# Attention output with features on partitions: values as loaded operand, two query tiles of scaled and turned weights as moving operand

## The chip, the core and the metric

The kernel runs on one core of one Trainium2 chip. The metric is the device time of a whole execution in microseconds. Before the change three runs took 3046.93, 3048.78 and 3053.7 us, median 3048.78.

The names of the engines in the profile are PE (TensorE: matrix products and transposes), PEld (its weight loads), ACT (ScalarE), DVE (VectorE), POOL (GpSimd) and SP (the engine that issues most transfers).

## The reference, cut to what matters

The program is a two-layer backbone over 512 tokens of width 1024 with a context of 256 tokens. Layer 0 mixes tokens by attention of 8 heads, layer 1 by pooling; each layer is followed by a product-key expert network, which takes most of the time. The change is in the attention alone:

```python
def one(qblk):                       # a block of 128 queries, all heads
    sc = einsum('bqhd,bkhd->bhqk', qblk, k) * scale      # 768 keys: 512 tokens + 256 of context
    p = softmax(sc, axis=-1)
    return einsum('bhqk,bkhd->bqhd', p, v)               # v: 128 features a head
y = concat_of_heads @ mla_w_o[j]     # (512 x 1024) @ (1024 x 1024)
x = layernorm(alpha * x + gate * y)
```

## The kernel before

**Stages.** `mla` (L212) first computes the latent projections, the rotary keys and the values `vt` (tokens on partitions, 6 chunks of 128 tokens, 1024 columns: 8 heads of 128 features). Then comes the attention loop, then the output projection with normalisation (`o_turn`, `y_tile`, `y_norm`), then the routing of the expert network.

**The attention loop** runs over 32 steps, head by head, four query tiles t of 128 queries to a head. The order of the work is the order of the code: each engine takes its instructions in the order in which they are issued here, and waits at an instruction whose operands are not there. For step i the code issues:

- `turn_p(i)`: six transposes of the unnormalised weights P (128 queries x 768 keys) into PSUM (`pt`), and one ScalarE copy to `PT` (keys on partitions);
- `scores(i+2)`: ten products into a PSUM tile `s` (two buffers), then on VectorE the row maximum into `mx` and its scaling;
- `projection(i)`: for query tiles 3, 0 and 1, a part of the next head's queries or keys (PSUM tile `qk`), split by ScalarE (high part) and VectorE (low part) into `qn` or `kn`; query tile 2 has none;
- `weigh(i)`: six f32 products PT x values into `po` (128 queries x 128 features), the reciprocal of the row sum, and a ScalarE copy to O with that factor;
- `soft(i+2)`: on ScalarE the exponential P of the scores, with the row sum in `mx`;
- for query tile 2 `head_split(h+2)`: the weights `hw` of the head after next are split, high part on ScalarE, low part on VectorE; the first product that needs them is that of query tile 3;
- `unit()`, mostly two to a step: a modulation dot of 128x1024 on VectorE (line L229, tile `wmod`), whose end lets SP fetch a later one.

**Behind the loop**, `o_turn(t)` transposes a query tile of O (queries on partitions) in eight products to features on partitions, and ScalarE and VectorE split it into the two halves OT. `row_form` makes a row `grow` of the gate. `y_tile` multiplies OT by the output weights `wo`, which are split on the way in the first tile. In the loop over t, `o_turn(t + 1)` stands ahead of `y_tile(t)`.

The functions that the change touches, with the lines of the profile:

Of the kernel before, what the change touches and what calls it, by code (L numbers as in the profile page):

```python
# [10 lines left out]
F32 = mybir.dt.float32  # L11
# [5 lines left out]
AF = mybir.ActivationFunctionType  # L17
# [4 lines left out]
D = 1024  # L22
S = 512
C = 256
L = S + C
NT = S // 128
H = 8
# [24 lines left out]
def body(ctx: ExitStack, tc, A):  # L52
    nc = tc.nc
# [6 lines left out]
    ident = const.tile([128, 128], F32, name="ident")  # L60
# [29 lines left out]
    def mm(out, lhsT, rhs, first, last):  # L90
        nc.tensor.matmul(out, lhsT, rhs, start=first, stop=last)  # L91
# [7 lines left out]
    def split(hi, lo, src):  # L99
        nc.scalar.copy(hi, src)  # L100
        nc.vector.tensor_tensor(lo, src, hi.bitcast(F32), op=OP.subtract)  # L101
# [110 lines left out]
    def mla():  # L212
        scale = DK ** -0.5
# [27 lines left out]
        vt = m2.tile([128, L // 128, D], F32, name="vt")  # L241
# [205 lines left out]
        for tiles in ((4, 5), (0, 1, 2, 3)):  # L447
            for t in tiles:
                if t < NT:
                    b = zB[t // 2][:, t % 2 * 256:t % 2 * 256 + 192]  # L450
# [105 lines left out]
                wo[h] = mO.tile([128, D], F32, name="wo", bufs=4)  # L556
                nc.sync.dma_start(wo[h], A["mla_w_o"][h * 128:(h + 1) * 128, :])

        O = mO.tile([128, NT, D], F32, name="O")
        at = Pool("att")  # L560
        pa = Pool("psT", space=PS)
        steps = [(h, t) for h in range(H) for t in range(NT)]
# [17 lines left out]
        def soft(i):  # L580
            p, mx = Sx.pop(i), sums[i]
            P = Px[i] = at.tile([128, L], F32, name="P", bufs=3)
            nc.scalar.activation(P, p[:, :L], AF.Exp, scale=scale, bias=mx[:, 1:2], accum_out=mx[:, 2:3])

        def turn_p(i):
            P = Px.pop(i)
            pt = pa.tile([128, 1024], F32, name="pt")
            for k in range(L // 128):
                nc.tensor.transpose(pt[:, k * 128:(k + 1) * 128], P[:, k * 128:(k + 1) * 128], ident)
            PT = PTx[i] = at.tile([128, L // 128, 128], F32, name="PT", bufs=2)  # L590
            nc.scalar.copy(PT.rearrange("p a b -> p (a b)"), pt[:, :L])

        def weigh(i):
            h, t = steps[i]
            PT, mx = PTx.pop(i), sums.pop(i)
            po = pa.tile([128, 512], F32, name="po")[:, :128]
            for k in range(L // 128):
                mm(po, PT[:, k, :], vt[:, k, h * 128:(h + 1) * 128], k == 0, k == L // 128 - 1)
            nc.vector.reciprocal(mx[:, 3:4], mx[:, 2:3])
            nc.scalar.activation(O[:, t, h * 128:(h + 1) * 128], po, AF.Copy, scale=mx[:, 3:4])  # L600

        def projection(j):

# [5 lines left out]
        for i in range(2):  # L609
            scores(i)  # L610
            soft(i)
        done = 6
        for i, (h, t) in enumerate(steps):
            turn_p(i)
            if i + 2 < len(steps):
                scores(i + 2)
            projection(i)
            weigh(i)
            if i + 2 < len(steps):
                soft(i + 2)  # L620
            if t == 2:
                head_split(h + 2)
            if 6 <= i < 10:
                wo_load(i - 6)
            want = 6 + min(74 - NL, (i + 1) * (74 - NL) // 32)
            while done < want:
                unit()
                done += 1
# [36 lines left out]
        def o_turn(t):  # L665
            OT[t] = [wk.tile([128, H, 128], R32, name=f"OT{k}", bufs=2) for k in range(2)]
            for half in range(2):
                p = tr.tile([128, 512], F32, name="tr")
                for k in range(4):
                    c = half * 4 + k  # L670
                    nc.tensor.transpose(p[:, k * 128:(k + 1) * 128], O[:, t, c * 128:(c + 1) * 128], ident)
                split(*[x[:, half * 4:half * 4 + 4, :].rearrange("p a b -> p (a b)") for x in OT[t]], p)

        xn = {}

# [902 lines left out]
```

## Time and profile before

| | us |
|---|---|
| median of three runs | 3048.78 |
| the profiled execution | 3045.26 |
| its span, first to last instruction | 3043.5 |
| TensorE busy | 2944.9 (97%) |
| VectorE busy | 2397.6 (79%) |
| ScalarE busy | 1216.7 (40%) |
| GpSimd busy | 960.9 (32%) |

All times within an execution are counted from the start of the span. A row of the timeline gives start, duration, engine, line, operation, output and inputs with shapes and count; in square brackets stands how long the engine had been idle before it, and what it waited for. A product of f32 operands is listed as two passes (the products of the split halves, type fp32r in the program, as one); durations of products overlap, so the distance of two starts tells what one costs. A small ScalarE row ACTIVATION_READ_ACCUMULATOR behind an exponential is the moment at which its row sum is stored. The granted clock is a share of full speed: 1.00 is the 2.4 GHz level, 0.50 the 1.2 GHz level.

### The profile page before, as it was taken

Reading aid. Unit: us, or ns where it says so; the run is one execution under the profiler, and the core shown is the slowest. Engines: PE = TensorE matmul, PEld = TensorE weight load, DVE = VectorE, ACT = ScalarE, POOL = GpSimd, SP = SyncE. Lnnn points to the kernel's source line nnn. Section 1 sums busy time; section 2 is a strip of 40 time slices with the busy share of each in tenths; the row PEclk is TensorE's granted clock in tenths of the full one; section 3 lists DMA queues with packets and bytes.
Section 4 is the critical chain, followed back from the end, with each engine's and each line's share of the span. In section 5 each row is a group of like instructions: output and inputs, shape, how many; then the busy total and the mean of one; then the engine's idle time right before and its main releaser. Section 6 shows DMA issues by size and latency. Waiting matters only on the chain.

```text
span 3043.5 us, 44992 instructions
## 1 busy us (share of the span) xinstructions
PE 2944.9 (97%) x15364; PEld 2509.6 (82%) x15364; DVE 2397.6 (79%) x4921; ACT 1216.7 (40%) x2267; POOL 960.9 (32%) x1047
## 2 busy tenths in 40 slices
PE   7999998999999999999998999899999999999997
PEld 4787757889999999999986755888999999999986
DVE  7667798977778888888876378896787888888886
ACT  3444234544433333333334333554433333333333
POOL 0000344004344444444412134102344444444430
PEclk9999999999999999999999999999999999999998
DMA  7366522675699999999982321577499999999993
GB/s 260 111 227 214 203 68 73 257 256 186 223 323 324 332 332 319 332 328 324 347 304 82 145 91 59 186 259 231 146 321 325 332 324 331 327 328 324 322 338 137
DMA packets 351479, 756.98 MB, mean 249 GB/s; under 512 B 30336, under 2 KB 121600, under 8 KB 347792
## 3 DMA queue, kind: packets, MB, share of 16 engines
q1 hardware_dynamic: 270768, 423.21, 41.4%
q0 software_dynamic: 77024, 280.56, 26.6%
q10 hardware_dynamic: 3456, 50.33, 4.3%
q8 instruction: 120, 1.97, 0.3%
q14 instruction: 111, 0.91, 0.1%
HBM read 695.26 MB, written 58.72 MB: 248 GB/s over the span
## 4 chain that ended last, share of the span: by engine, by line
PE 83%; DVE 9%; issue 3%; ACT 2%; DMA 2%; POOL 0%; SPq 0%; ACTq 0%; DVEq 0%; POOLq 0%
PE acc L96 12%; PE acc L97 11%; PE acc L95 11%; PE mm L91 7%; PE pA L95 5%; PE pA L97 5%; PE pA L96 5%; PE pG L97 5%; PE pG L95 5%; PE pG L96 5%; DVE eq L1198 2%; DVE oh L1193 1%; PE po L91 1%; DVE lo L101 1%; PE s L91 1%
## 5 line engine op out<-in xcount | busy, mean ns | idle before, releaser
L101 DVE TENSOR_TENSOR lo<-raw,hi 128x512 fp32r<-128x512 f32 x1024 | 669.1, 692 | 276.0 <-ACT hi L100 273.9
L95 PE MATMUL acc<-hi,WH 128*128 128x512 f32 x1536 | 598.1, 389 | 5.4 <-ACT WH L1152 2.9
L97 PE MATMUL acc<-hi,WL 128*128 128x512 f32 x1536 | 601.9, 392 | 0.0
L96 PE MATMUL acc<-lo,WH 128*128 128x512 f32 x1536 | 601.4, 392 | 0.4 <-DVE lo L101 0.4
L100 ACT CAST hi<-raw 128x512 fp32r<-128x512 f32 x1024 | 586.4, 616 | 33.5 <-DMA raw<-in_peer_v_rows_dram 16.0
L1264 POOL DMA_INDIRECT flat<-in_peer_v_rows_dram,idx x256 | 335.2, 1309 | 437.8 <-DVE accg L1285 364.8
L1264 POOL DMA_INDIRECT flat<-in_peer_u_rows_dram,idx x256 | 331.2, 1294 | 436.3 <-DVE flat L1275 383.3
L1285 DVE SCALAR_TENSOR_TENSOR accg<-flat,wa,accg 128x1024 f32<-128x1024 f32 x254 | 325.6, 1282 | 39.3 <-DMA flat<-in_peer_v_rows_dram,idx 35.3
L97 PE MATMUL pG<-hH,lo 128*128 128x384 f32 x1024 | 345.8, 338 | 8.1 <-DVE lo L101 7.9
L1152 ACT CAST WH<-W 128x384 fp32r<-128x384 f32 x256 | 131.5, 514 | 555.2 <-PE acc L96 485.4
L95 PE MATMUL pA<-hH,hi 128*128 128x384 f32 x1024 | 346.6, 339 | 1.6 <-ACT hi L100 1.6
L95 PE MATMUL pG<-hH,hi 128*128 128x384 f32 x1024 | 347.1, 339 | 0.0
L97 PE MATMUL pA<-hH,lo 128*128 128x384 f32 x1024 | 344.1, 336 | 0.2
L96 PE MATMUL pG<-hL,hi 128*128 128x384 f32 x1024 | 344.0, 336 | 0.0
L96 PE MATMUL pA<-hL,hi 128*128 128x384 f32 x1024 | 343.2, 335 | 0.0
L95 PEld LDWEIGHTS acc<-hi,WH 128*128 128x128 f32 x1536 | 288.5, 188 | 62.1 <-ACT WH L1152 3.6
L97 PEld LDWEIGHTS acc<-hi,WL 128*128 128x128 f32 x1536 | 288.2, 188 | 61.0 <-DVE WL L1157 0.6
L96 PEld LDWEIGHTS acc<-lo,WH 128*128 128x128 f32 x1536 | 288.2, 188 | 57.5 <-DVE lo L101 1.3
L1275 DVE SCALAR_TENSOR_TENSOR flat<-flat,h2g 128x1024 f32<-128x1024 f32 x256 | 304.1, 1220 | 29.7 <-DMA flat<-in_peer_u_rows_dram,idx 28.8
L97 PEld LDWEIGHTS pG<-hH,lo 128*128 128x128 f32 x1024 | 193.2, 189 | 10.0 <-DVE lo L101 10.0
L95 PEld LDWEIGHTS pA<-hH,hi 128*128 128x128 f32 x1024 | 192.6, 188 | 6.2 <-ACT hi L100 2.3
L91 PE MATMUL mm<-h2T,wq 128*128 128x512 f32 x448 | 196.9, 592 | 0.0
(377 smaller groups left out, 4376.5 us busy)
## 6 DMA issues: line engine op xcount, KB each, us to landing
raw<-in_peer_uT_dram SPq DMA_DIRECT2D x512, 256.0 KB, 6.1
raw<-in_peer_v_rows_dram SPq DMA_DIRECT2D x512, 256.0 KB, 6.5
gates<-flat ACTq DMA_DIRECT2D x24, 2048.0 KB, 7.4
gb<-gates SPq DMA_DIRECT2D x58, 768.0 KB, 11.4
wmod<-in_w_mod_dram SPq DMA_DIRECT2D x84, 512.0 KB, 4.4
wq<-in_peer_w_q_dram SPq DMA_DIRECT2D x32, 512.0 KB, 3.7
wo<-in_w_mod_dram SPq DMA_DIRECT2D x12, 512.0 KB, 5.2
gb<-gates POOLq DMA_DIRECT2D x6, 768.0 KB, 9.9
```

The source lines that it names most:

```text
L91: nc.tensor.matmul(out, lhsT, rhs, start=first, stop=last)
L95: nc.tensor.matmul(out, a[0], b[0], start=first, stop=False)
L96: nc.tensor.matmul(out, a[0], b[1], start=False, stop=False)
L97: nc.tensor.matmul(out, a[1], b[0], start=False, stop=last)
L100: nc.scalar.copy(hi, src)
L101: nc.vector.tensor_tensor(lo, src, hi.bitcast(F32), op=OP.subtract)
L1152: nc.scalar.copy(wh, Wt[b])
L1193: nc.vector.tensor_tensor(o1.rearrange("p t (i k) -> p t i k", k=2), I1T[:, ts, None, :].to_broadcast([128, GT, 64, 2]), line.rearrange("p ...
L1198: nc.vector.tensor_tensor(eq, I2T[:, None, ts].to_broadcast([128, 128, GT]), rep, op=OP.is_equal)
L1264: nc.gpsimd.indirect_dma_start(out=r, out_offset=None, in_=A["peer_u_rows"] if i < NSEL else A["peer_v_rows"], in_offset=bass.IndirectOffs ...
L1275: nc.vector.scalar_tensor_tensor(r, r, 1.0, h2g, op0=OP.mult, op1=OP.mult, accum_out=aa[:, i:i + 1])
L1285: nc.vector.scalar_tensor_tensor(accg[0], r, wa[:, k:k + 1], accg[0], op0=OP.mult, op1=OP.add)
```

## The change

The weights P are scaled by the reciprocal of their row sum before they are transposed, not after the product with the values: the reciprocal now stands in `soft`, directly behind the exponential, and a new function `even` scales P in place on ScalarE. The turned weights of two query tiles lie side by side in one tile PT of 256 queries. `weigh` does nothing at even t; at odd t it multiplies with the values as loaded operand (`lhsT`) and the 256 queries as moving operand, and a plain copy brings the result, features on partitions, to O (128 x 8 heads x 512 queries). `o_turn` no longer transposes: it splits O directly.

```diff
-        O = mO.tile([128, NT, D], F32, name="O")
+        O = mO.tile([128, H, S], F32, name="O")
...
             P = Px[i] = at.tile([128, L], F32, name="P", bufs=3)
             nc.scalar.activation(P, p[:, :L], AF.Exp, scale=scale, bias=mx[:, 1:2], accum_out=mx[:, 2:3])
+            nc.vector.reciprocal(mx[:, 3:4], mx[:, 2:3])
+
+        def even(i):
+            if i < len(steps):
+                nc.scalar.activation(Px[i], Px[i], AF.Copy, scale=sums.pop(i)[:, 3:4])
 
         def turn_p(i):
...
-            PT = PTx[i] = at.tile([128, L // 128, 128], F32, name="PT", bufs=2)
-            nc.scalar.copy(PT.rearrange("p a b -> p (a b)"), pt[:, :L])
+            h, t = steps[i]
+            if t % 2 == 0:
+                PTx[0] = at.tile([128, L // 128, 256], F32, name="PT", bufs=2)
+            nc.scalar.copy(PTx[0][:, :, t % 2 * 128:(t % 2 + 1) * 128], pt[:, :L].rearrange("p (a b) -> p a b", b=128))
 
         def weigh(i):
+
             h, t = steps[i]
-            PT, mx = PTx.pop(i), sums.pop(i)
-            po = pa.tile([128, 512], F32, name="po")[:, :128]
+            if t % 2 == 0:
+                return
+            po = pa.tile([128, 512], F32, name="po")[:, :256]
             for k in range(L // 128):
-                mm(po, PT[:, k, :], vt[:, k, h * 128:(h + 1) * 128], k == 0, k == L // 128 - 1)
-            nc.vector.reciprocal(mx[:, 3:4], mx[:, 2:3])
-            nc.scalar.activation(O[:, t, h * 128:(h + 1) * 128], po, AF.Copy, scale=mx[:, 3:4])
+                mm(po, vt[:, k, h * 128:(h + 1) * 128], PTx[0][:, k, :], k == 0, k == L // 128 - 1)
+            nc.scalar.copy(O[:, h, (t - 1) * 128:(t + 1) * 128], po)
...
         for i in range(2):
             scores(i)
             soft(i)
+        even(0)
         done = 6
         for i, (h, t) in enumerate(steps):
             turn_p(i)
+            even(i + 1)
             if i + 2 < len(steps):
                 scores(i + 2)
...
             for half in range(2):
-                p = tr.tile([128, 512], F32, name="tr")
-                for k in range(4):
-                    c = half * 4 + k
-                    nc.tensor.transpose(p[:, k * 128:(k + 1) * 128], O[:, t, c * 128:(c + 1) * 128], ident)
-                split(*[x[:, half * 4:half * 4 + 4, :].rearrange("p a b -> p (a b)") for x in OT[t]], p)
+                hs = slice(half * 4, half * 4 + 4)
+                split(*[x[:, hs, :] for x in OT[t]], O[:, hs, t * 128:(t + 1) * 128])
```

ScalarE at the start of the loop, before (L583 is the exponential, L591 the copy PT, L600 the copy to O):

```order
L583 ACT_TABLE_LOAD
L583 ACTIVATE P,mx<-s,mx 128x768 x2
L591 COPY PT<-pt 128x768
L100 CAST kn_873<-qk 128x512
L600 ACTIVATE O<-po,mx 128x128
L583 ACTIVATE P,mx<-s,mx 128x768
L591 COPY PT<-pt 128x768
```

and after (L588 is `even`, L598 the copy PT):

```order
L583 ACT_TABLE_LOAD
L583 ACTIVATE P,mx<-s,mx 128x768 x2
L588 ACTIVATE P<-P,mx 128x768
L598 COPY PT<-pt 128x6x128
L588 ACTIVATE P<-P,mx 128x768
L100 CAST kn_873<-qk 128x512
L583 ACTIVATE P,mx<-s,mx 128x768
```

Between the two first exponentials and the first copy PT stands a scaling, and the next step's scaling stands directly behind each copy PT.

VectorE from query tile 1 of the first head to query tile 3, before (L576 and L577 are the maximum and its scaling, L599 the reciprocal, L229 the dots):

```order
L101 TENSOR_TENSOR kn_874<-qk,kn_873 128x256
L599 RECIPROCAL mx<-mx 128x1
L229 SCALAR_TENSOR_TENSOR wmod,mcol_82<-wmod,sc_c 128x1024 x2
L576 TENSOR_REDUCE mx<-s 128x1
L577 TENSOR_SCALAR mx<-mx 128x1
L599 RECIPROCAL mx<-mx 128x1
L101 TENSOR_TENSOR hw_1048<-hw,hw_1047 128x640
L229 SCALAR_TENSOR_TENSOR wmod,mcol_82<-wmod,sc_c 128x1024 x2
L576 TENSOR_REDUCE mx<-s 128x1
```

and after (L584 is the reciprocal):

```order
L101 TENSOR_TENSOR kn_874<-qk,kn_873 128x256
L584 RECIPROCAL mx<-mx 128x1
L229 SCALAR_TENSOR_TENSOR wmod,mcol_82<-wmod,sc_c 128x1024 x2
L576 TENSOR_REDUCE mx<-s 128x1
L577 TENSOR_SCALAR mx<-mx 128x1
L584 RECIPROCAL mx<-mx 128x1
L101 TENSOR_TENSOR hw_1037<-hw,hw_1036 128x640
L229 SCALAR_TENSOR_TENSOR wmod,mcol_82<-wmod,sc_c 128x1024 x2
L576 TENSOR_REDUCE mx<-s 128x1
```

The order of these rows is the same; what the reciprocal reads is another: before the row sum of step i, whose exponential was issued two steps earlier, after that of step i+2, whose exponential is issued in this step, behind the copy to O.

## Rows read from the trace of the kernel before

**Rows 1.** The page, part 4: the chain that ended last, by engine.

```profile
PE 83%; DVE 9%; issue 3%; ACT 2%; DMA 2%; POOL 0%; SPq 0%; ACTq 0%; DVEq 0%; POOLq 0%
```

**Rows 2.** Stretches: length, busy us (instructions) of each engine, granted clock, DMA share, GB/s.

```profile
142.00:162.00 20.00, 20.00 (x125) 16.07 (x125) 14.05 (x30) 9.65 (x20) 0.00 (x0) 1.00 0.63 218
```

**Rows 3.** TensorE's waits up to 400 us: waiter, releaser, total us, times, longest.

```profile
PE po L91 <- ACT PT L591: 2.3, 2, 1.4
PE tr L158 <- ACT nr L143: 2.3, 1, 2.3
```

**Rows 4.** Timeline of TensorE: passes of f32 products of 128 and 512 columns.

```profile
153.64 1.50 PE L91 MATMUL po<-vt,PT 128*128 128x128 f32 x12
154.98 0.82 PE L589 MATMUL pt<-ident,P 128*128 128x128 f32 x6
...
1693.73 14.95 PE L91 MATMUL tr<-flat 128*128 128x512 f32 x32
```

**Rows 5.** Groups of VectorE, 122 to 292 us: busy, mean ns, idle before, releaser.

```profile
L229 DVE SCALAR_TENSOR_TENSOR wmod<-wmod,sc_c 128x1024 f32<-128x1024 f32 x62 | 73.2, 1214 | 1.1 <-DMA wmod<-in_w_mod_dram 1.1
L576 DVE TENSOR_REDUCE mx<-s 128x1 f32<-128x768 f32 x30 | 28.7, 956 | 24.0 <-PE s L91 24.0
...
L101 DVE TENSOR_TENSOR hw<-hw,hw 128x640 fp32r<-128x640 f32 x6 | 5.0, 826 | 13.3 <-ACT hw L100 13.3
```

**Rows 6.** Timeline, query tiles 1 to 3 of the second head.

```profile
154.66 1.21 DVE L229 SCALAR_TENSOR_TENSOR wmod<-wmod,sc_c 128x1024 f32<-128x1024 f32 x1
...
155.45 0.90 ACT L583 ACTIVATE P<-s,mx 128x768 f32<-128x768 f32 x1
...
155.79 1.22 DVE L229 SCALAR_TENSOR_TENSOR wmod<-wmod,sc_c 128x1024 f32<-128x1024 f32 x1
...
156.23 0.20 ACT L583 ACTIVATION_READ_ACCUMULATOR P<-s,mx 128x1 f32 x1
156.32 0.80 ACT L591 COPY PT<-pt 128x768 f32<-128x768 f32 x1
...
158.07 1.60 PE L91 MATMUL po<-vt,PT 128*128 128x128 f32 x12
...
160.85 0.72 ACT L100 CAST hw<-hw 128x640 fp32r<-128x640 f32 x1
...
162.59 0.50 PE L95 MATMUL qk<-cqT,hw 128*128 128x512 f32 x1
```

**Rows 7.** Timeline, the start of the loop.

```profile
120.50 0.96 DVE L576 TENSOR_REDUCE mx<-s 128x1 f32<-128x768 f32 x1 [1.38 <-PE s L91]
121.29 0.19 ACT L583 ACTIVATION_READ_ACCUMULATOR P<-s,mx 128x1 f32 x1
...
121.54 0.87 PE L589 MATMUL pt<-ident,P 128*128 128x128 f32 x6 [1.08 <-ACT P L583]
121.74 0.90 ACT L583 ACTIVATE P<-s,mx 128x768 f32<-128x768 f32 x1 [0.25 <-DVE mx L577]
```

**Rows 8.** Timeline, the end of the loop and the first output products.

```profile
284.30 0.82 PE L589 MATMUL pt<-ident,P 128*128 128x128 f32 x6
...
291.33 0.37 ACT L600 ACTIVATE O<-po,mx 128x128 f32<-128x128 f32 x1 [1.70 <-PE po L91]
...
292.50 2.05 ACT L100 CAST OT<-tr 128x512 fp32r<-128x512 f32 x4 [0.80 <-PE tr L671]
...
296.74 0.51 PE L95 MATMUL y<-wo,OT 128*128 128x512 f32 x1 [1.62 <-ACT wo L100]
```

**Rows 9.** Stretches around idle times of TensorE; columns as in rows 2.

```profile
101.00:104.00 3.00, 0.63 (x3) 0.19 (x1) 2.50 (x8) 0.38 (x1) 0.00 (x0) 1.00 0.77 235
...
108.00:109.00 1.00, 1.00 (x4) 0.71 (x4) 0.99 (x3) 0.00 (x0) 0.00 (x0) 0.50 0.48 33
...
119.50:122.00 2.50, 1.42 (x9) 1.09 (x10) 1.11 (x2) 2.23 (x4) 0.00 (x0) 1.00 0.00 0
...
298.00:304.00 6.00, 6.00 (x14) 4.74 (x15) 4.57 (x4) 3.05 (x4) 0.00 (x0) 0.50 0.86 288
```

## The prediction

> **What bounds the kernel now.** I read the chain that ended last first: TensorE has 83% of it [rows 1], so what matters is what TensorE does or waits for. The attention loop lies at about 115 to 292 us, the output projection behind it up to about 360. In the table of stretches TensorE is busy for 20.00 of 20 us in mid-loop, ScalarE for 9.65 [rows 2]: the loop is paced by TensorE alone. The list of waits agrees: TensorE loses 2.3 us (in two waits) at the loop's end to the copy PT and 2.3 us in the projection, where it waits for the normalised row tile nr [rows 3]; before the first transposes `pt` it idles 1.08 us [rows 7]. So a microsecond of TensorE work saved in the loop is a microsecond saved, and a wait put on it there is one lost, unless it falls into the last of these.
>
> **TensorE's own work.** Before, each step has 6 products `po` of 128 columns, twelve passes in the trace since each f32 product takes two; they start at 153.64 and the next transposes at 154.98, so 1.34 us, 0.112 a pass [rows 4]. After, a pair of steps has twelve passes of 256 columns: the same columns, half the weight loads. The nearest row for a wider f32 product is 512 columns, 32 passes in 14.95 us, 0.467 each with gaps (0.91 ns a column; 0.112 for 128 is 0.87) [rows 4]. So the cost goes by the columns, and what can go is only what stands above the columns' rate. I take 0.215 a pass, 2.58 us a pair against 2.68, a gain of 0.10; interpolated between the two rows it would be 0.230, 2.76, a loss of 0.08. Sixteen pairs: **-1.6 us**, ends -1.6 and +1.3.
>
> The Trainium skill, page "TensorE: Matmul & The Clock Gate", section "LDWEIGHTS (loading the stationary operand)", gives a weight load of 128 columns as 128/1.2, an estimate of 107 ns, which by itself would account for the 0.112; the section on the issue gap has 262 cycles for 256 columns, some 109 ns. By these a pair would take some 1.3 us. The 512-column row, at four times the time of a 128-column pass and not twice, speaks against it.
>
> **ScalarE and VectorE in the loop.** Added: 32 in-place scalings `even` of 128x768 on ScalarE. No such row exists; the copy PT of this size without a scale takes 0.80, the exponential with scale and bias from a tile 0.90 [rows 6]; I take 0.90. Sixteen output copies of 128x256 replace 32 of 128x128, which gives back some 6 us of ScalarE. That ScalarE total (9.65 of 20 us now) stays below its limit, so the sum of durations costs nothing. What costs is order, at three places.
>
> *The start.* `even(0)` stands behind both first exponentials on ScalarE, and the reciprocal of step 0 stands in front of the maximum of step 1 on VectorE. Before, the accumulator of the first exponential is read at 121.29 (0.19), TensorE transposes at 121.54; the second maximum had run at 120.50 to 121.46, beside it, and the second exponential started at 121.74 [rows 7]. After: accumulator 121.48, reciprocal to 121.6, second maximum 121.6 to 122.56, its scaling to 122.73, second exponential 122.83, even(0) behind it (0.78 + 0.10 later, from the spacing in [rows 6]) at 123.71 to 124.61, first transposes at 124.67. TensorE is behind them in order: **+3.1 us**.
>
> *Each head.* The new reciprocal waits for the exponential of its own step, and two modulation dots (154.66 and 155.79, 1.13 apart, [rows 6]) and the next maximum are queued behind it on VectorE. Let T be the start of the transposes of query tile 2, the shortest step (no projection, and now no `po`). By the rows behind T = 154.98 [rows 4, 6]: output copy, then the exponential at T+0.47, accumulator T+1.25 to T+1.45, reciprocal T+1.5, two dots to T+3.84 (the scores that the maximum needs are there at T+3.2), maximum 0.99 to T+4.83, its scaling T+4.98, next exponential T+5.08, and behind it on ScalarE the head split hw, T+5.96 to T+6.68; the VectorE half (0.82, [rows 5]) T+6.7 to T+7.53. TensorE needs two times transposes and scores, 3.09 each (154.98 to 158.07), and asks for hw at T+6.18 (even(i+1) ends at T+2.95, just in time for T+3.09). It waits 0.56 for the high half and 0.40 for the low half in its third product. Before, hw was cast at 160.85 and first used at 162.59 [rows 6], 1.0 us after it was ready. Tile 2 of six heads casts one: 6 x 0.96 = **+5.8 us**. Bounds: 0, if the dots or the copies come a microsecond sooner than these spacings say; and more, if a dot also waits for its load (the 62 dots wait 1.1 us in all now).
>
> *The end.* Without projections nothing covers PT -> po. From the transposes of step 30 to the end of the last output copy it was 284.30 to 291.70, 7.40 us [rows 8]. After: T+0.47 exponential, accumulator T+1.25, PT copy T+1.35, even(31) T+2.05 to T+2.95, transposes T+3.0 to 3.83, PT copy to T+4.67, po 2.58 + 0.16 to T+7.5, copy to T+7.9: +0.5. Steps 27 and 29 likewise reach `po` before their PT copy, which stands behind an exponential held up by the same dots, by 0.6 to 0.7 each: **+1.8 us** together, ends +0.5 and +2.5.
>
> **The projection.** Thirty-two transposes of O go. The first sixteen stood on the path: O ended at 291.70, the first cast OT began at 292.50 and the products y at 296.74 [rows 8]; now the casts follow the output copy on ScalarE directly, -0.8, and read 512 values from SBUF instead of PSUM, a few hundredths each: **-0.7 us**. The other sixteen (0.9 us for eight) end in the 2.3 us that TensorE waits for nr [rows 3], which hangs on VectorE's work since the end of the first y: nothing.
>
> **The clock.** After TensorE had been idle for over 2 us of 101 to 104 the granted clock fell to the 1.2 GHz level about 2 us after it resumed (0.50 at 108 to 109), for some 3.3 us; the 1.1 us idle at 120.5 did not lower it; at the end it fell at 298 to 304 [rows 9]. The new 4.2 us idle at the start should lower it: 3.3 us at half speed lose **+1.6 us** (0 to 3.3). At the end, where the clock fell before too, an idle of 2.5 us comes earlier and may catch the last po: **+0.8** (0 to 1.6).
>
> **Sum.** -1.6 + 3.1 + 5.8 + 1.8 - 0.7 + 1.6 + 0.8 = +10.8. The profiled execution took 3045.26 (span 3043.5) and lies 3.5 below the median of the three runs, 3048.78; its sum is 3056.1. I add the difference to the median: **3059.6 us**, its own range 3056 to 3063. Behind 360 us I let it pass one to one: TensorE holds the chain there.
>
> **Rivals.**
> - *The head waits do not form.* For: the walk rests on waits under 1 us, and VectorE's maxima wait 24.0 us for scores now [rows 5], so there is slack to move. Against: it is the dots behind the reciprocal that use this slack up. Then +10.8 - 5.8 = +5.0, about 3053.8.
> - *Weight loads set the po passes.* If 0.112 is the load and 256 columns hide under one too, a pair takes 1.34 us and the sixteen pairs give 21.4 in place of 1.6. The longer waits at even and PT in the then shorter steps take some 3 us back; +10.8 - 19.8 + 3 = -6.0, 3042.8: not slower. It decides as soon as the passes lie below 0.16. The 512-column row speaks against it. This is the rule of the Trainium skill's page "TensorE: Matmul & The Clock Gate" named above.
> - *The clock falls at every head.* Each head gets a gap of about 1 us; should six more falls follow, 6 x 1.6 = 9.6, 3069. Against: the single gap of 1.1 us did nothing [rows 9].
>
> **Chances.** Forecast 0.66, no head waits 0.17, weight loads 0.08, clock at every head 0.09. What a measurement can tell from no change is 0.2%, 6.1 us, so up to 3054.9 it is "the same". Slower: the forecast nearly whole (0.63), and the clock case: 0.72. Same: no head waits mostly (0.15), the rest of the forecast, part of the weight loads: 0.20. Faster: 0.08. The range takes the forecast and the case without head waits, and part of the way to the clock case: 3051 to 3065.
>
> **What would show it.** First transposes near 124.7 with even as releaser; a wait of TensorE on hw (ScalarE, then VectorE) of about 1 us at tile 3 of six heads; passes of po 0.21 to 0.23 apart; `even` at 0.8 to 0.95; y starting 4.2 us after the last output copy. It is wrong if VectorE's maximum does not start later after the transposes of tile 2, or if po passes come at 0.11.

## The result and the profile after

The changed kernel takes 3065.23 us (median of 6 runs, 3062.72 to 3068.64), the kernel before 3046.2 (median of 6, 3044.55 to 3053.7). The ratio is 1.0058, 95% interval 1.0048 to 1.0068, so some 15 to 21 us slower. The forecast was slower, at 3059.6; the sign was right, the size too small, and 3065.23 lies just above the range's end of 3065. (The forecast added 10.8 us to 3048.78, the median of the three runs known then; on the median of six it would be 3057.0.) The profiled execution took 3066.88, span 3065.1.

The chain that ended last, by engine, after [rows 1]:

```profile
PE 81%; DVE 10%; issue 3%; ACT 3%; DMA 2%; POOL 0%; SPq 0%; ACTq 0%; DVEq 0%; POOLq 0%
```

TensorE's waits up to 400 us (waiter, releaser, total us, times, longest), after [rows 3]:

```profile
PE tr L158 <- ACT nr L143: 7.1, 3, 5.2
PE pt L594 <- ACT P L588: 6.4, 2, 4.2
...
PE qk L95 <- ACT hw L100: 3.9, 7, 1.1
...
PE po L91 <- ACT PT L598: 2.0, 3, 0.9
```

Where one row of waits stood for nr and one for PT, there are now waits for the scaled P (its 4.2 is the start, 2.2 the end), for the split weights hw of a head, and three times as much for nr behind the loop.

Start of the loop, after [rows 7] (L583 exponential, L584 reciprocal, L588 `even`, L594 first transposes):

```profile
122.94 0.19 ACT L583 ACTIVATION_READ_ACCUMULATOR P<-s,mx 128x1 f32 x1
123.17 0.17 DVE L584 RECIPROCAL mx<-mx 128x1 f32<-128x1 f32 x1 [2.40 <-ACT P L583]
123.25 0.94 DVE L576 TENSOR_REDUCE mx<-s 128x1 f32<-128x768 f32 x1
...
124.47 0.90 ACT L583 ACTIVATE P<-s,mx 128x768 f32<-128x768 f32 x1 [1.33 <-DVE mx L577]
...
125.36 0.92 ACT L588 ACTIVATE P<-P,mx 128x768 f32<-128x768 f32 x1
...
126.34 1.54 PE L594 MATMUL pt<-ident,P 128*128 128x128 f32 x6 [4.21 <-ACT P L588]
```

This is the predicted order. The first transposes come 4.8 us later than before, but the first projection `qk` of a head, ahead of all the change's work, stood at 112.84 before and at 114.56 here; in the profiles below it lies between 111.5 and 115.0 for the same code. So stage times are counted from it: 11.78 against 8.70, the change's part 3.1 us. TensorE then ran at the 1.2 GHz level (granted clock 0.50 up to 129 us and 0.62 from there to 132; before 1.00), "the lower clock" from here on; stretches as in rows 9:

```profile
126.00:129.00 3.00, 2.66 (x10) 2.34 (x10) 0.00 (x0) 1.37 (x3) 0.00 (x0) 0.50 0.00 0
129.00:132.00 3.00, 3.00 (x9) 1.69 (x8) 0.20 (x1) 0.55 (x1) 0.00 (x0) 0.62 0.00 0
```

TensorE and what it waits for, the third query tile of a head into the fourth, after [rows 4, 6]:

```profile
137.08 2.75 PE L91 MATMUL po<-PT,vt 128*128 128x256 f32 x12
139.67 0.82 PE L594 MATMUL pt<-ident,P 128*128 128x128 f32 x6
...
145.66 0.71 ACT L100 CAST hw<-hw 128x640 fp32r<-128x640 f32 x1
...
146.40 0.83 DVE L101 TENSOR_TENSOR hw<-hw,hw 128x640 fp32r<-128x640 f32 x1 [0.45 <-ACT hw L100]
...
146.42 0.50 PE L95 MATMUL qk<-cqT,hw 128*128 128x512 f32 x1 [0.46 <-ACT hw L100]
...
146.76 0.40 PE L96 MATMUL qk<-cqT,hw 128*128 128x512 f32 x1
...
147.28 0.19 PEld L97 LDWEIGHTS qk<-cqT,hw 128*128 128x128 f32 x1 [0.56 <-DVE hw L101]
...
169.41 0.50 PE L95 MATMUL qk<-cqT,hw 128*128 128x512 f32 x1 [0.46 <-ACT hw L100]
```

Two things are read here. A pass of `po` takes (139.67 - 137.08) / 12 = 0.216 us, 2.59 a pair. And TensorE stands for 0.46 us before the first product with hw and again some 0.3 before the third, until VectorE's half is done: the weight load of the third starts 0.52 us behind the second product, where such products follow each other at 0.23. From one head to the next it is 169.41 - 146.42 = 22.99 us; before 22.24 (162.59 [rows 6] to the next such row at 184.83).

End of the loop, after [rows 8] (the first two rows are the products of steps 27 and 29):

```profile
284.41 2.86 PE L91 MATMUL po<-PT,vt 128*128 128x256 f32 x12 [0.54 <-ACT PT L598]
...
293.93 2.86 PE L91 MATMUL po<-PT,vt 128*128 128x256 f32 x12 [0.53 <-ACT PT L598]
296.62 0.82 PE L594 MATMUL pt<-ident,P 128*128 128x128 f32 x6
299.67 0.87 PE L594 MATMUL pt<-ident,P 128*128 128x128 f32 x6 [2.23 <-ACT P L588]
301.43 4.54 PE L91 MATMUL po<-PT,vt 128*128 128x256 f32 x12 [0.89 <-ACT PT L598]
...
306.01 0.37 ACT L608 COPY O<-po 128x256 f32<-128x256 f32 x1 [4.63 <-PE po L91]
...
310.43 0.49 PE L95 MATMUL y<-wo,OT 128*128 128x512 f32 x1 [2.90 <-ACT wo L100]
```

The last product takes 4.54 instead of the 2.86 of the two before it: the lower clock caught it (granted clock 0.60 from 303 to 306 us).

Behind the loop stands what the prediction had at nothing. A normalised row tile nr goes to TensorE, which transposes it, and to GpSimd, which makes two passes over it. The low halves of the turned output (VectorE, L101), GpSimd's passes (L148, L149), VectorE's dots (L229) and next norm (L124), and TensorE's transposes of nr (L158), timeline after:

```profile
331.37 2.39 POOL L148 TENSOR_TENSOR xo<-nr,ln 128x1024 f32<-128x1024 f32 x1 [326.76 <-DMA wo<-in_w_mod_dram]
...
331.82 5.29 DVE L101 TENSOR_TENSOR OT<-O,OT 128x512 fp32r<-128x512 f32 x2 [1.82 <-ACT OT L100]
...
333.84 2.72 POOL L149 TENSOR_TENSOR xo<-xo,ln 128x1024 f32<-128x1024 f32 x1
...
337.04 1.21 DVE L229 SCALAR_TENSOR_TENSOR wo<-wo,sc_c 128x1024 f32<-128x1024 f32 x1
...
346.91 1.22 DVE L124 TENSOR_TENSOR nr<-y,grow 128x1024 f32<-128x1024 f32 x1
...
353.01 1.86 PE L158 MATMUL tr<-ident,nr 128*128 128x128 f32 x8 [5.15 <-ACT nr L143]
...
371.36 3.36 DVE L229 SCALAR_TENSOR_TENSOR wo<-wo,sc_c 128x1024 f32<-128x1024 f32 x1
...
380.79 1.09 PE L158 MATMUL tr<-ident,nr 128*128 128x128 f32 x8 [1.81 <-ACT nr L143]
```

The same place before:

```profile
317.97 2.39 POOL L148 TENSOR_TENSOR xo<-nr,ln 128x1024 f32<-128x1024 f32 x1 [313.35 <-DMA wo<-in_w_mod_dram]
...
318.38 1.29 DVE L101 TENSOR_TENSOR OT<-tr,OT 128x512 fp32r<-128x512 f32 x2 [1.78 <-ACT OT L100]
...
319.59 1.86 DVE L229 SCALAR_TENSOR_TENSOR wo<-wo,sc_c 128x1024 f32<-128x1024 f32 x1
...
321.38 3.40 DVE L229 SCALAR_TENSOR_TENSOR wo<-wo,sc_c 128x1024 f32<-128x1024 f32 x1
...
332.45 1.22 DVE L124 TENSOR_TENSOR nr<-y,grow 128x1024 f32<-128x1024 f32 x1
...
338.54 1.97 PE L158 MATMUL tr<-ident,nr 128*128 128x128 f32 x8 [2.29 <-ACT nr L143]
```

Before, the source was the PSUM tile `tr`, and two low halves beside GpSimd took 1.29 us; what GpSimd slowed were the dots behind them, 1.86 and 3.40. Now the source is O, in SBUF, and the two halves take 5.29, as long as GpSimd's two passes last, while the dots behind them take 1.21. From the start of the halves to the next norm VectorE needs 346.91 - 331.82 = 15.09 us, before 332.45 - 318.38 = 14.07: of the 4.0 us on the halves only 1.0 is new, the rest was paid on the dots before.

TensorE waits 5.15 us for nr instead of 2.3, but of these 2.9 us only 0.8 are VectorE's delay. Counted from the first `y` (310.43, before 296.74 [rows 8]), TensorE begins to wait at 37.4 us where it was 39.5, as the transposes of O are gone, and nr comes at 42.58 where it was 41.80. The saved transposes fall into the wait, and the rest of the loss comes behind it. The fourth tile's products end 1.3 us later than before (more of them at the lower clock, and a wait of 0.3 for the second pair of low halves, which takes 5.25). Ahead of the last norm a dot runs beside GpSimd's passes and takes 3.36 where it took 1.21, and TensorE waits 1.81 us for the last nr; before, these transposes waited for nothing. They start 70.36 us behind the first `y`, before 66.70.

### The stages of all kernels

From the rows of each profile, us: first transposes, last product `po` (start, end) and first routing product `mm<-kT`, counted from the first `qk`; one head to the next in mid-loop; first `y` to first routing product; and the timed ratio to the kernel before.

| | pt | head to head | last po | y to routing | routing | ratio (95%) |
|---|---|---|---|---|---|---|
| before | 8.70 | 22.25 | 176.85, 178.45 | 73.69 | 257.59 | 1 |
| after | 11.78 | 22.99 | 186.87, 191.41 | 77.40 | 273.27 | 1.0058 (48 to 68) |
| scale | 11.80 | 22.25 | 182.19, 183.79 | 73.21 | 264.17 | 1.0036 (23 to 49) |
| early | 11.23 | 22.99 | 185.64, 189.94 | 77.04 | 271.44 | 1.0048 (30 to 66) |
| dots | 11.79 | 22.3 | 182.58, 185.44 | 77.50 | 267.38 | 1.0039 (24 to 54) |
| early_dots | 9.88 | 22.4 | 179.81, 184.35 | 77.35 | 266.15 | 1.0031 (20 to 41) |
| shift | 11.78 | 22.10 | 179.54, 182.40 | 77.69 | 264.83 | 1.0030 (17 to 44) |
| nopool_after | 11.79 | 22.99 | 186.88, 191.42 | 68.48 | 264.36 | 1.0032 (20 to 44) |
| nopool_before | 8.65 | 22.25 | 176.80, 178.40 | 69.74 | 253.59 | 0.9990 (0.9981 to 0.9999) |
| ahead | 11.78 | 22.98 | 188.62, 194.11 | 74.94 | 273.50 | 1.0050 (34 to 65) |
| direct | 11.77 | 22.99 | 188.65, 194.14 | 76.15 | 276.74 | 1.0053 (38 to 68) |
| best | 9.87 | 22.10 | 176.93, 181.47 | 75.58 | 260.90 | 1.0021 (12 to 30) |
| best2 | 9.84 | 23.4 | 194.76, 199.01 | 69.16 | 275.13 | 1.0059 (45 to 73) |
| best3 | 9.84 | 22.64 | 183.47, 188.49 | 70.44 | 262.76 | 1.0014 (05 to 23) |

Intervals give the last digits of the ratio. By routing the change has cost 273.27 - 257.59 = 15.7 us.

### The profile page after: what moved, and what is told of

Read it like the earlier page. It is cut to its first block, busy times and chain, and to the rows that moved or that the text cites. A ratio compares the mean times of both kernels' runs of the same rounds, so it can differ in the third digit from the quotient of the medians.

```text
span 3065.1 us, 44537 instructions
## 1 busy us (share of the span) xinstructions
PE 2952.6 (96%) x15140; PEld 2503.7 (82%) x15140; DVE 2405.5 (78%) x4921; ACT 1240.4 (40%) x2283; POOL 961.7 (31%) x1047
## 4 chain that ended last, share of the span: by engine, by line
PE 81%; DVE 10%; issue 3%; ACT 3%; DMA 2%; POOL 0%; SPq 0%; ACTq 0%; DVEq 0%; POOLq 0%
PE acc L96 11%; PE acc L97 11%; PE acc L95 11%; PE mm L91 7%; PE pA L95 5%; PE pA L97 5%; PE pG L97 5%; PE pA L96 5%; PE pG L95 5%; PE pG L96 5%; DVE eq L1205 2%; DVE oh L1200 2%; PE po L91 1%; DVE lo L101 1%; PE y L96 1%
## 5 line engine op out<-in xcount | busy, mean ns | idle before, releaser
L101 DVE TENSOR_TENSOR lo<-raw,hi 128x512 fp32r<-128x512 f32 x1024 | 669.6, 694 | 273.7 <-ACT hi L100 263.5
```

## The experiments

### scale: the scaling pass alone, in the kernel before

```diff
+            nc.vector.reciprocal(mx[:, 3:4], mx[:, 2:3])
+
+        def even(i):
+            if i < len(steps):
+                nc.scalar.activation(Px[i], Px[i], AF.Copy, scale=sums.pop(i)[:, 3:4])
...
-            nc.vector.reciprocal(mx[:, 3:4], mx[:, 2:3])
-            nc.scalar.activation(O[:, t, h * 128:(h + 1) * 128], po, AF.Copy, scale=mx[:, 3:4])
+            nc.scalar.copy(O[:, t, h * 128:(h + 1) * 128], po)
```

> The kernel before, with the weights scaled by the row sum's reciprocal on ScalarE ahead of the transposes and the output copied without a scale: the product of weights and values stays as it was, 32 products with the weights as loaded operand. It takes the change's scaling pass alone. Theory (the start and the scaling pass's place on ScalarE cost most of it, and the clock falls behind the longer start): first transpose 11.8 us after the first projection as with the change, attention ends 5 to 9 us later than before (hand estimate 3.9 us with no clock loss, and 1.6 to 3 us of clock), and the turned layout's own part is the rest of the change's 13 us. Rival (the layout is what costs, by the 2.6 us products at every second step): attention ends less than 4 us later than before. Neither expects the low halves behind attention to be slowed, since they come from PSUM here: from the end of attention to the first routing product as in the kernel before.

TensorE at the start and at its first product:

```profile
123.41 1.54 PE L594 MATMUL pt<-ident,P 128*128 128x128 f32 x6 [4.21 <-ACT P L588]
...
130.27 1.50 PE L91 MATMUL po<-vt,PT 128*128 128x128 f32 x12
```

`even` is called where the change calls it. First transposes +3.1; first `po` at 130.27 - 111.61 = 18.66, before 13.33 (+5.33, so 2.2 us by the lower clock); last `po` +5.34. A head takes 22.25 us as before: 32 scaling passes of 0.95 us cost the running loop nothing, their price is the start and its clock. Theory, and at 5.34 us near the low end of its 5 to 9. What neither side expected is 1.7 us between the last `po` and the first `y` (7.17 us, before 5.45): the last modulation dot ends at 298.03, 2.3 us behind the last copy to O, and the gate's row `grow` and the first split of `wo` stand behind it. Up to routing this kernel is 6.6 us above the kernel before; timed it is 7 to 15 us, and the rest is not explained.

### dots: reciprocals behind the dots

```diff
-            nc.vector.reciprocal(mx[:, 3:4], mx[:, 2:3])
...
+        def turn_sum(i):
+            nc.vector.reciprocal(sums[i][:, 3:4], sums[i][:, 2:3])
...
                 unit()
                 done += 1
+            if i + 2 < len(steps):
+                turn_sum(i + 2)
```

> The changed kernel, with VectorE's reciprocal of a step issued behind that step's dot products instead of ahead of them, so that ScalarE's scaling pass has to wait longer for it and the low halves of the next head stand elsewhere in VectorE's row. Theory (at each head's fourth step the high and low halves of the projected q come late, as ScalarE and VectorE do them behind the exponential, the scaling pass and the reciprocal): the wait of TensorE for the halves at the heads shrinks, and the loop ends 2 to 4 us earlier than with the change, worked out by hand from the durations of its trace (5.95 instead of 9.7 us above before, clock apart). Rival (the heads' waits come from ScalarE's high half alone): the loop ends within 1 us of the change's end, or later, since the scaling pass now waits for the dots.

The same place as in the rows after, third query tile into the fourth:

```profile
141.91 0.72 ACT L100 CAST hw<-hw 128x640 fp32r<-128x640 f32 x1
...
142.66 0.83 DVE L101 TENSOR_TENSOR hw<-hw,hw 128x640 fp32r<-128x640 f32 x1 [1.73 <-ACT hw L100]
...
142.81 0.50 PE L95 MATMUL qk<-cqT,hw 128*128 128x512 f32 x1
...
143.14 0.40 PE L96 MATMUL qk<-cqT,hw 128*128 128x512 f32 x1
...
143.54 0.19 PEld L97 LDWEIGHTS qk<-cqT,hw 128*128 128x128 f32 x1 [0.44 <-DVE hw L101]
```

The wait for the high half is gone, one of some 0.2 for the low half remains (143.54 - 143.14, less 0.23; the 0.44 in the row is idle time of the weight loads alone); most heads take 22.3 us instead of 22.99. The last `po` starts 4.3 us earlier than in the changed kernel (its end 6.0, since it also ran at the full clock), more than the 2 to 4 of the theory. What stood behind the reciprocal on VectorE did hold up the heads.

### shift: the product of a pair one step later

```diff
-            weigh(i)
+            if i:
+                weigh(i - 1)
...
+        weigh(len(steps) - 1)
         while queue:
```

> The changed kernel, with the product of a pair of tiles issued one step later (at the next pair's first step, ahead of nothing that waits for it), so that neither ScalarE's copy of the transposed tile nor the product itself stands between a head's projections and its scores. Theory (what the loop loses behind its start is waits at the odd steps and the heads, which the product of both tiles, 2.6 us in one piece at every second step, sets): TensorE's waits for the transposed tile vanish and the loop ends 5 to 8 us earlier than with the change, by hand from the durations of its trace. Rival (ScalarE, with 0.96 us more in each of 32 steps, sets the loop's pace whatever the order): it ends less than 2 us earlier.

(The tile PT is kept by the number of its pair, not shown.) The last `po` starts 7.3 us earlier and ends 9.0 earlier, the end beyond the theory's 5 to 8, since it ran at the full clock. A head takes 22.10: the product now lies in the third tile's step, where TensorE reached hw too early, and covers the split. With no wait left, 22.10 against 22.25 before shows what the wider product saves, 0.15 us a head, and 22.99 - 22.10 = 0.89 what the waits cost. Theory; ScalarE does not set the pace.

### early, and early_dots: the first scaling ahead of the second exponential

```diff
         for i in range(2):
             scores(i)
-            soft(i)
-        even(0)
+        soft(0)
+        even(0)
+        soft(1)
```

> The changed kernel, with the first step's scaling pass issued on ScalarE ahead of the second exponential. Theory (the start's 3.1 us are the order of ScalarE's instructions: the first scaling pass stands behind the exponential of step 1): the first transpose comes about 9.8 us after the first projection of a head (8.7 before, 11.8 with the change), and TensorE, idle for less time, keeps its clock there; attention ends 2 to 3.6 us earlier than with the change, and the whole stands at about 1.0047 of the kernel before, where the change stands at 1.0058. Rival (ScalarE's added pass of 0.96 us per step is what the loop as a whole pays): the first transpose moves as above, but the end of attention stays within 1 us of the change's.

In this profile TensorE idled 2.30 us before the first `qk` (waiting for a split of the first head, work ahead of the change) and ran the next products at the lower clock, 0.63 us each instead of 0.39. So 11.23 does not tell the order from the clock, and the end of attention, 1.5 us earlier, lies between theory and rival. It was repeated together with the edit of dots.

> The changed kernel with two edits, each run before alone: the first scaling pass ahead of the second exponential, and the reciprocals behind the dot products. Theory (the start and the heads' waits are separate losses and add): first transpose 9.8 us after the first projection where the clock is full there, no wait of TensorE for the halves of q at the heads, and the loop's end 1.5 to 3 us ahead of that with the reciprocals alone (172.2 us behind the first projection), so 169 to 170.7 us, counted to the end of the last product: 2 to 0.5 us above nothing but the kernel before's 165.6 plus the clock. In numbers from the first projection itself: 178.45 before, 183.7 with the reciprocals alone, 180.7 to 182.2 here; behind attention as in the change (77 to 77.7 us). Rival (with the reciprocals late, the first scaling pass is not what holds the start): end of attention within 1 us of 183.7.

(Its last numbers, from the first projection, are the ones to compare.) TensorE at the start and the first `po`:

```profile
122.01 1.54 PE L598 MATMUL pt<-ident,P 128*128 128x128 f32 x6 [2.27 <-ACT P L592]
...
131.99 2.75 PE L91 MATMUL po<-PT,vt 128*128 128x256 f32 x12
```

First transposes 9.88, 1.9 us sooner than in dots; first `po` 19.86 against 22.46; last `po` starts 2.8 sooner. Its end, 184.35, misses the expected 180.7 to 182.2, as this last product fell into the lower clock again (4.54). By the number alone it lies within 1 us of 183.7, where the rival had it. But dots itself ends at 185.44 in the table, and the start, which the rival denies, did come 1.9 us sooner. The start and the heads add up, as the theory says. That TensorE would keep its clock at the start, as expected of early, did not come: behind the shorter idle of 2.27 us the granted clock is 0.50 from 122 to 125 us.

### nopool_after, nopool_before: without GpSimd's passes

```diff
-            affine(wk, xn[t], ln, x_mid[0][:, t, :], (nc.gpsimd, nc.gpsimd))
+            nc.gpsimd.dma_start(x_mid[0][:, t, :], xn[t])
```

> The changed kernel without GpSimd's two passes (L148, L149) over each normalized row tile behind attention; the gain and bias of that norm are left out, and the rows are written as they are. Theory (VectorE's low halves of the turned output run beside GpSimd's passes, both now reading and writing SBUF, and are slowed four times): the two groups of low halves that took 5.3 us take 1.3 to 1.6 us each, and from the first product with the output weights to the first product of the routing it is 73 to 74.5 us, where the change takes 77.4 and the kernel before 73.7. Rival (the SBUF source or the strided read of O itself is slow): they stay at 4 us or more, and the stretch at 76 us or more.

> The kernel before with the same left out: GpSimd's two passes per tile behind attention and with them that norm's gain and bias. It says what GpSimd's passes cost where the low halves come from PSUM. Theory (a source in PSUM is hardly touched by GpSimd; only the dots, which read SBUF, are): low halves 1.2 to 1.3 us for two as in the kernel before, and the stretch from the first product with the output weights to the first routing product 72 to 73.7 us, so that the change's part in this stretch shrinks from 3.7 to under 1 us. Rival (GpSimd's passes slow VectorE alike whatever the source): the stretch shrinks here by as much as in the changed kernel, 3 us or more, and the change's part stays near 3.7 us.

Both kernels leave out that norm's gain and bias with the passes, so the values behind it differ; only times are read from them. VectorE's groups of low halves between 290 and 400 us (busy, mean ns, idle before), after:

```profile
L101 DVE TENSOR_TENSOR OT<-O,OT 128x512 fp32r<-128x512 f32 x8 | 13.0, 1680 | 3.6 <-ACT OT L100 3.6
```

after, without GpSimd's passes:

```profile
L101 DVE TENSOR_TENSOR OT<-O,OT 128x512 fp32r<-128x512 f32 x8 | 5.1, 688 | 3.7 <-ACT OT L100 3.6
```

before, with them:

```profile
L101 DVE TENSOR_TENSOR OT<-tr,OT 128x512 fp32r<-128x512 f32 x8 | 5.1, 684 | 3.7 <-ACT OT L100 3.7
```

The strided SBUF source by itself costs nothing (688 ns against 684). From the first `y` to routing the changed kernel falls from 77.40 to 68.48, the kernel before from 73.69 to 69.74: the change's part goes from +3.7 to -1.3. Both stretches shrank more than expected, since GpSimd also slows the dots there (the 3.40 above, 1.22 without it). Timed, the change costs 1.0032 - 0.9990 = 0.0042 instead of 0.0058, 4.9 us less; the traces say 5.0. From the intervals of the three ratios the timed figure is uncertain by some 5.5 us, so it is the traces that carry this. The theory on the low halves is shown, and that GpSimd's passes make up the change's loss in this stretch; its sizes were low. The kernel before shrinks by 3.95 us, past the 3 us that the rival named, but not by as much as the changed one (8.92).

### ahead: low halves before GpSimd starts

```diff
         o_turn(0)
+        o_turn(1)
         for t in range(NT):
-            if t + 1 < NT:
-                o_turn(t + 1)
...
             y = y_tile(t)
+            if t + 2 < NT:
+                o_turn(t + 2)
```

> The changed kernel with the splits of a tile of the output issued one tile earlier: tiles 0 and 1 before the products, tile t+2 right behind the products of tile t and ahead of its norm. The low halves then run before GpSimd begins its passes or between them, at the price of standing ahead of the norm on VectorE. Theory (GpSimd's passes slow the low halves): the four low halves behind the first products take 1.3 to 1.6 us a pair instead of 5.3 for the first of them, and the stretch from the first product with the output weights to the first routing product is 74 to 77 us (77.4 with the change: 3.9 us less in the low halves, 0.5 to 3 us more where the norm waits for them). Rival (what GpSimd slows is all that VectorE does in this stretch, so that work moved within it is slowed wherever it stands): 77 us or more.

VectorE and GpSimd behind the first tile's products:

```profile
327.88 1.30 DVE L101 TENSOR_TENSOR OT<-O,OT 128x512 fp32r<-128x512 f32 x2 [2.26 <-ACT OT L100]
...
335.23 3.16 POOL L148 TENSOR_TENSOR xo<-nr,ln 128x1024 f32<-128x1024 f32 x1 [330.61 <-DMA xr<-in_x_dram]
...
336.06 3.41 DVE L229 SCALAR_TENSOR_TENSOR wo<-wo,sc_c 128x1024 f32<-128x1024 f32 x1
```

The low halves take 1.30 again, the stretch 74.94 us: theory. The dots now stand beside GpSimd and take 3.41 each, so part of the rival holds as well. The whole is hardly better (1.0050, intervals overlap). In this profile the loop, the changed kernel's code, had a longer spell at the lower clock (first `po` at 24.27 instead of 22.52; the last took 5.49 us), which used up what the stretch gained.

### direct, best, best2, best3: repairs

```diff
-            nc.scalar.copy(O[:, h, (t - 1) * 128:(t + 1) * 128], po)
+            split(*[x[:, h, (t - 1) * 128:(t + 1) * 128] for x in O], po)
...
+            OT[t] = [x[:, :, t * 128:(t + 1) * 128] for x in O]
```

O is a pair of tiles here, high and low half. best adds the edits of early and shift, best2 those of early and dots; best3 that of early, splits hw at the second tile (`if t == 1`) and issues the low half of `po` behind the dots. direct and best have three buffers for wo, best2 and best3 four.

> The changed kernel with the turned output split into its high and low halves where it leaves PSUM: ScalarE copies po to the high half, VectorE subtracts it from po, and no pass over O is left behind attention (P in two buffers and the output weights in three instead of four make the room). Theory (behind attention the passes over O cost the change 4 us by GpSimd and hold up the first product): the first product with the output weights comes 1.5 to 3.5 us behind the last product of attention where it is 4.5 us with the change, and from there to the first routing product 72 to 74.5 us instead of 77.4; together 4.5 to 8 us less than the change. Rival (what stands behind attention is bound by the output weights' own splits and loads, with three buffers all the more): less than 2 us.

> Three edits together: the first scaling pass ahead of the second exponential, the product of a pair one step later, and the split where the output leaves PSUM. Theory (these are the three places where the change lost its time): start about 1 us above before instead of 3.1, loop as in the kernel with the later product, and behind attention 4.5 to 8 us less than the change: 2.5 us below to 3 us above the kernel before, ratio 0.9992 to 1.001, against 1.0058 of the change. Rival (VectorE's 16 low halves in the loop, and ScalarE's scaling, bind the loop when TensorE no longer waits): the loop ends 4 us or more later than in the kernel with the later product alone, ratio 1.002 or more.

> The changed kernel with three edits: the first scaling pass ahead of the second exponential, the reciprocals behind the dots, and the output split where it leaves PSUM, with four buffers of output weights again (room by two buffers of P and one of the turned weights). Theory: the loop as in the run with the first two edits, the first product with the output weights 4 to 5 us behind the last product of attention, and from there to the first routing product 70 to 73 us, as the low halves are gone from there and the first tile's products no longer wait for loads as in the kernel with three buffers (75.6 there, of which 4 us on the first tile): in all 3 us below to 2 us above the kernel before, ratio 0.999 to 1.0007. Rival (VectorE, with the 16 low halves in the loop and the dots behind them, is late at the end of attention, and the one buffer of turned weights makes ScalarE wait for the products): ratio above 1.0015.

> The changed kernel with three edits against the three losses, chosen after the runs before: the first scaling pass ahead of the second exponential; the halves of the next head's weights split one step earlier (at a head's second step instead of its third), with the reciprocals left where the change has them; and the output split where it leaves PSUM, VectorE's low half behind the step's dots, where nothing waits for it (P in two buffers, turned weights in one, output weights in four). Theory (each loss has its own cause, so that all three go): first transpose 9.9 us after the first projection, no wait for the halves of q, end of the last product 180 to 184 us after the first projection (178.45 before, 191.4 with the change, 183.2 with the first scaling pass and late reciprocals), 4 to 7 us from there to the first product with the output weights, and 69 to 71 us from that to the first routing product (73.7 before, 77.4 with the change, 69.2 with the split at PSUM and late reciprocals); from first projection to first routing product 254 to 261 us against 257.6 before: ratio 0.9985 to 1.0015. Rival (VectorE, with the dots, the low halves of the output and those of the projections, is full in the loop: its queue is late for the maxima): attention ends later than 186 us and the ratio is 1.002 or more.

direct went as its rival: the gap from the last `po` to `y` grew to 6.5 us, and the first tile of `y` took 16.8 us instead of 14.8. best kept shift's loop (last `po` 0.1 us from the kernel before), but with three buffers the first tile of `y` waited for wo and took 19.2 us against 15.1; the ratio, 1.0021, is the rival's, its mechanism is not. best2 has the shortest stretch behind attention, 69.16 us, and the worst loop: in its trace VectorE's low half of `po` waits 1.6 us on average for ScalarE's high half, with the dots and then the late reciprocals queued behind it. What the fewer buffers of P and PT add to that, no run separates. TensorE's waits in best3, up to 400 us:

```profile
PE pt L594 <- ACT P L588: 7.6, 8, 2.3
```

The earlier split of hw moved the wait to the scaled P, some 0.5 us at each of six heads: the split stands ahead of the copy PT and the next scaling on ScalarE. 22.64 us a head. The stretch behind attention came as expected (70.44), but attention ends at 188.5, as in the rival. The ratio, 1.0014, lies in the theory's range and not in the rival's; the 262.76 us to routing miss the theory's 254 to 261. No version beats the kernel before.

## Why the prediction was right in sign and short in size

Its terms against the runs, us:

| term | predicted | measured | from |
|---|---|---|---|
| po passes | -1.6 | -1.2 | 8 heads x 0.15 (shift) |
| start | +3.1 | +3.1 | 11.78 - 8.70 |
| clock at the start | +1.6 | +2.2 | scale |
| heads, six waits | +5.8 | +5.3 | 6 x 0.89 (after, shift) |
| end of the loop | +1.8 | +1.9 | what is left of 12.96 |
| clock at the last po | +0.8 | +1.7 | 4.54 - 2.86 |
| last po to y | -0.7 | -1.0 | 4.46 - 5.45, from the end of po |
| y to routing | 0 | +3.7 | 77.40 - 73.69 |
| sum to routing | +10.8 | +15.7 | |

The walk through the loop held: the order of ScalarE at the start, the place and the size of the heads' waits (0.46 and 0.3 us, forecast 0.56 and 0.40), the end (0.54 and 0.53 before the products of steps 27 and 29, forecast 0.6 to 0.7 each). From the transposes of step 30 to the last copy's end it is 306.38 - 296.62 = 9.76 us, 8.1 without the 1.7 of the clock, against 7.40 before: +0.7, forecast +0.5. The rival by which the heads' waits don't form is out (0.89 us each), and that of weight loads too (0.216 us a pass; it needed under 0.16). The clock did not fall at every head: 1.00 in the stretch below, and in those that follow up to 290 us,

```profile
140.00:160.00 20.00, 19.41 (x96) 14.11 (x95) 14.65 (x28) 12.21 (x21) 0.00 (x0) 1.00 0.52 175
```

where TensorE is busy 19.41 of 20 us, not 20.00 [rows 2]. Its two falls at start and end were sized 1.5 us too small together: at the start the clock was low already when TensorE resumed, and stayed so for some 5 us (126.3 to 131.3, from the two stretches shown), not 3.3.

The step that failed is in the projection: "The other sixteen (0.9 us for eight) end in the 2.3 us that TensorE waits for nr [rows 3], which hangs on VectorE's work since the end of the first y: nothing." That the saved transposes bring nothing here held: they fall into that wait. What failed is the nothing for VectorE's work, on which the wait hangs, and for the tiles behind it. The change lengthened that work: the low halves read SBUF instead of PSUM ("a few hundredths each" was said of the casts alone) and stand beside GpSimd's passes, 5.3 us for two instead of 1.3. The step looked at what goes from TensorE, not at what the new source does to the engine that TensorE waits for. That GpSimd's passes are the cause is shown by the two kernels without them, the stretch then being 1.3 us shorter than before instead of 3.7 longer. How the 3.7 come about is read from the rows: 0.8 us at the first wait, since there the dots are spared what the halves pay, and the other 2.9 on the last two tiles.

The Trainium skill, page "SBUF — State Buffer", section "Who interferes with whom", states it: a VectorE instruction with two SBUF inputs contends with a GpSimd instruction that reads SBUF, one with a single SBUF input, outside VectorE's two-port modes, does not, and the port pair that the two engines share is an exclusive lock. The traces agree: 1.29 us with one input in PSUM, 5.29 with both in SBUF, and in the second case VectorE ends at 337.1, some 0.5 us behind GpSimd's second pass. The prediction had not weighed this rule.

Open: the timed difference is 14.6 to 20.7 us and the trace's up to routing 15.7. From routing to the end the profiles take between 2673 and 2678 us: 2673.1 for the kernel before and 2674.0 without GpSimd's passes, 2677.3 for the changed kernel, 2673.3 for best3, 2675.1 to 2678.0 for the others. In the changed kernel none of its 4.2 us arise in the first 1260 us behind routing, where the two profiles run within 0.1 us of each other, and nearly all in the second layer's expert network, whose code is the same. Whether this follows from the change or is chance of two executions is not settled.

## What to carry to other kernels

When a source moves from PSUM to SBUF, look at what GpSimd does at that time: an operation that costs the same alone may take four times as long beside it, and the price is due wherever somebody waits for VectorE. Look too at what GpSimd slowed there before: here the dots, so that three of four lost microseconds were no new loss at the first wait. A pass added to an engine with half its time free was free in the running loop; it cost where the pipeline fills and drains and where another instruction was queued just behind it, so walk those places instruction by instruction. A saving of operations on an engine counts only after the waits that the shorter step uncovers: here 0.15 us a head was saved and 0.89 paid.

## What the runs showed of the hardware that was not expected

Two VectorE subtractions of 128x512 f32 take 1.29 us with a source in PSUM, even beside GpSimd's passes, and 1.30 with a source in SBUF without them; beside them, with an SBUF source, 5.29. A dot of 128x1024 with both inputs in SBUF goes from 1.22 to 3.41 beside such passes. GpSimd's passes beside the halves took 2.39 and 2.72 us. And the spell at the lower clock behind the same idle of 4.2 us was not always equally long: with the same instructions up to there the first `po` came at 22.5 us in the profiles of after and nopool_after, and at 24.3 in ahead, where the granted clock was 0.50 from 126 to 132 us and still 0.52 from 132 to 135.
